# Two more pairs of k-tiles of an output projection by seven products, with three block sums made in an earlier stage

## The chip, the cores and the metric

The kernel runs on one core of a Trainium2 chip. The metric is the device time of one execution in microseconds (us). Times given for a kernel are medians of several executions; a profile shows one execution.

A core has engines that run side by side, each with its own fixed order of instructions: TensorE (PE, matmuls), VectorE (DVE), ScalarE (ACT), GpSimd (POOL) and SyncE (SP), which here issues the DMAs. An instruction waits on semaphores for what it needs, and everything behind it on its engine waits with it.

## The reference, cut to what matters

One layer of an encoder on 256 positions of width 2048, in float32. An input projection gives the inputs of a state-space mixer (SSD: a convolution over 5 positions, decays, two directions) and of a pooling mixer. Both results, 1024 wide each, go side by side through one output projection; then come a gated feed-forward stage and a gated embedding.

```python
hn = rmsnorm(h, mix_norm_pre[i])
proj = hn @ w_in[i]
z, xbc, dt_raw, u = jnp.split(proj, split_at, axis=-1)
y_ssd = ssd_mixer(z, xbc, dt_raw, ...)
y_pool = pool_mixer(u, pool_w[i], pool_scale[i])
mix = jnp.concatenate([y_ssd, y_pool], axis=-1) @ w_out[i]
h = h + rmsnorm(mix, mix_norm_post[i])
hn = rmsnorm(h, ffn_norm_pre[i])
ff = conv_glu(hn, w_ffn_up[i], ffn_conv_w[i], ffn_conv_b[i], w_ffn_down[i])
h = h + rmsnorm(ff, ffn_norm_post[i])
gate = jax.nn.sigmoid(rmsnorm(h, ple_norm_pre[i]) @ w_ple_gate[i])
h = h + rmsnorm(gate * (p[i] @ w_ple[i]), ple_norm_post[i])
```

The change concerns the product with `w_out`, which is 2048 x 2048.

## The kernel before

**Products in two parts.** Every operand of a large product is split in a rounded part and the rest (`split`, L141): ACT copies the weights to the rounded type (L152, names ending in h), DVE subtracts (L153, names ending in l). A product is then three matmuls: h by h, l by h and h by l. Weights come from DRAM into one of three buffers of 1 MB (`raw`, L156) and are split in two blocks of 1024 elements a partition. Activations are put into panels in the same two parts (`put`, L187: ACT L190, DVE L191).

**Stages.** First dt and u (dtu), then the three xbc slabs in the order 2, 0, 1 (`xbc`, L639): each multiplies 512 columns of `w_in` (`feature_major`, L323: four loads, u 0 to 3, of two blocks each), scales the result (xr, L411), does the convolution on ACT (L422) and DVE (L428, sixteen steps), and finishes with a tanh (L645) and L647. Then z, the output projection (wo), the embedding's product ple and the feed-forward stage (ug is its first weight, ga the result).

**Work laid aside.** `work` is a list of lists of small jobs; `aside` (L196) takes one list behind each load's matmuls. The lists for the slabs stand at L695 to L728: the pooling mixer (mx and mixt at L597 to L604, pw), the decays (dps and dec), the segment sums (`seg_sums`, L568: cps, seg_h L575, seg_c L576, and eight scalings seg_x and seg_w, L579 and L580), the segment matrices (`seg`, L582: two matmuls, then E by L588 on ACT, L589 on DVE, L590 on ACT), and others. The softplus of dt (sp, L530 to L541) and da come just before slab 2's lists.

**Who sets the order.** The program is written in Tile: a scheduler orders the instructions of each engine when the program is built, from the dependences, the buffers that come free and its own estimate of times; `issue_after` adds a few edges. The order in the text of the program is therefore not the order on an engine.

**Seven products.** A pair of k-tiles times a half (1024 columns) of `w_out` is a 2 x 2 product of blocks. The usual way takes eight block products, 24 matmuls of 128 x 512. `seven_products` (L239) takes seven, 21 matmuls, with sums of blocks of the weights (`add_blocks`, L232: DVE L235, L236, L237) and of the activations (`Sums`, L785, made once for each k and kept in `got`). The results gather in the usual four accumulators and four more, which `combine` (L269) adds up one pair behind the last fast one. The weights are split as a, b, c and d (L251 to L260): a and b are plain blocks, c and d hold sums. The sums are made in place in the raw buffer, or, if `block_sums` (L208) made them earlier, read back from DRAM into a page; in that case the raw buffer gets only 1536 of its 2048 columns. `block_sums` returns four lists of jobs: load, nothing, additions, store.

**The output projection.** `sublayer` (called at L852) runs two halves of 1024 columns over eight pairs, u 0 to 7, in the order k = 8, 10, 12, 14, 0, 2, 4, 6. The lower k need y, which is turned by `y_turn` (L758, four jobs set aside at L766) while the upper four pairs run. Before the change pair u 5 (k 2) of half 0 and pairs u 2 and 4 (k 12 and 0) of half 1 are fast, all three with sums in place. At the end the norm: squares on ACT (L822), products with the gain (L823), the updates of h (L830) and the new panel (wox) by PE transposes and `put`.

**Buffers.** Pages (1 MB) come from a pool of 13, raw buffers from one of 3, split parts from pools of 5.

Of the kernel before, what the change touches and what calls it, by code (L numbers as in the profile page):

```python
# [36 lines left out]
V_MIX, V_SCW, V_SCB, V_SN, V_PS, V_FN = 0, 16, 76, 88, 96, 104  # L37
# [14 lines left out]
def build(nc, a, out):  # L52
    x = a["x"][0]
    w_in, w_out, w_up = a["w_in"][0], a["w_out"][0], a["w_ffn_up"][0]
# [3 lines left out]
    with tile.TileContext(nc) as tc, \  # L58
# [12 lines left out]
        def page(name, dtype=F32):  # L71
            return gp.tile([P, 2048], dtype, tag="pg", bufs=13, name=name)
# [43 lines left out]
        def load(dst, src, ahead=False):  # L116

            with tc.issue_after(last["dma"]) if last and not ahead else nullcontext():
                return ins(nc.sync.dma_start(dst, src))
# [36 lines left out]
        def raw(name, src, a_, b_):  # L156
            r = wp.tile([P, 2048], F32, tag="raw", bufs=3, name=name)
            if src is None:
                return r
            last["dma"] = load(r[:, :a_ * b_].rearrange("p (a b) -> p a b", a=a_), src, True)  # L160
            return r
# [43 lines left out]
                yield o, c  # L205
                c += o.shape[-1]

        def block_sums(name, w, c0, k, held):  # L208


            pg = []

            def fetch():
                r = page(f"{name}b{c0}_{k}")
                pg.append(r)
                load(r.rearrange("p (k c) -> p k c", k=2),
                     w[k * P:(k + 2) * P, c0:c0 + 1024].rearrange("(k p) c -> p k c", p=P))

            def add():
                add_blocks(pg[0])  # L220
                if held:
                    sums_[name, c0, k] = pg[0], True

            def store():
                if not held:
                    t = dp.tile([P, 2048], F32, tag=f"{name}s{c0}_{k}", bufs=1, name=f"{name}s{c0}_{k}")
                    load(t, pg[0])
                    sums_[name, c0, k] = t, False

            return [fetch], [], [add], [store]  # L230

        def add_blocks(r):  # L232

            v = r.rearrange("p (b c) -> p b c", b=4)
            nc.vector.tensor_add(v[:, 0:2], v[:, 0:2], v[:, 1::2])  # L235
            nc.vector.tensor_add(v[:, 3], v[:, 3], v[:, 0])  # L236
            nc.vector.tensor_add(v[:, 2], v[:, 2], v[:, 3])  # L237
# [124 lines left out]
        def rms(name, parts, scale, n=1):  # L362

            base = EPS
            for i, q in enumerate(parts):
                m = tiny(f"{name}m{i}", n)
                nc.gpsimd.tensor_scalar(m, q, scale, base, op0=ALU.mult, op1=ALU.add)
                base = m
            r = tiny(f"{name}r", n)
            nc.gpsimd.tensor_tensor(r, m, mhalf[:, :n], op=ALU.pow)  # L370
            return r
# [71 lines left out]
        for u in range(0, NK, 2):  # L443
            r = [wp.tile([P, 2048], F32, tag="raw", bufs=3, name=f"dtur{u}") if u else r0, page(f"dtur{u + 1}")]
            for j in range(2):
                k = u + j
# [17 lines left out]
            for j in range(2):  # L464
                k = u + j
# [127 lines left out]
        cat = Panel.__new__(Panel)  # L593
# [97 lines left out]
        def job(f, *args):  # L691
            return lambda: f(*args)

        xd = {}
        work.extend([  # L695
            [],
            [job(pool_mix, 0), job(pool_mix, 1)],
            [job(pool_mix, 2), job(pool_mix, 3), job(decays), job(seg_sums)],
            [job(seg, 0), job(seg, 1)],
        ])  # L700
        bc = xbc(2)
        work.extend([
            [job(seg, 2), job(pool_map, 0), job(pool_map, 1)],
            [job(cb, bc, 0), job(cb, bc, 1), job(seg, 3)],
            [job(seg, 4), job(weigh, 0, 0), job(pool_map, 2)],
            [job(seg, 5), job(pool_map, 3)],
# [30 lines left out]
        for t in range(2):  # L737
# [13 lines left out]
            r = rms(f"yn{t}", [ss], rz[t][:, 1:2], n=2)  # L751
# [16 lines left out]
        def gload(name, src):  # L768
            g = cp.tile([P, D], F32, tag="gain", name=name)
            load(g, src.partition_broadcast(P))  # L770
            return g
# [33 lines left out]
        def sublayer(name, w, ks, get, gain, h, vnext, panel=Panel, fast=((), ()), sums=None, at=()):  # L805

            mg = [page(f"{name}m{t}") for t in range(2)]
            sq = [[], []]
            for half in range(2):

                alt = main(f"{name}s{half}") if fast[half] and half == 0 else []
                acc = [main(f"{name}a{half}{t}") for t in range(2)]
                if fast[half]:
                    alt += main(f"{name}s{half}") if half else []
                token_major(f"{name}{half}", w, half * 1024, ks, get, acc, 1, fast[half], alt, sums, at if half else ())
                for t in range(2):
                    for n in range(2):
                        q = tiny(f"{name}q{t}{half}{n}", 1)
                        junk = sp.tile([P, 512], F32, tag="junk", bufs=1, name=f"{name}j{t}{half}{n}")
                        c = slice(half * 1024 + n * 512, half * 1024 + (n + 1) * 512)  # L820
                        b = acc[t][n]
                        nc.scalar.activation(junk, b, AF.Square, accum_out=q)  # L822
                        nc.vector.tensor_mul(mg[t][:, c], b, gain[:, c])  # L823
                        sq[t].append(q)
            r = [rms(f"{name}{t}", sq[t], 1.0 / D) for t in range(2)]
            pan = panel(f"{name}x")
            for c in range(4):
                s = slice(c * 512, (c + 1) * 512)
                for t in range(2):
                    nc.vector.scalar_tensor_tensor(h[t][:, s], mg[t][:, s], r[t], h[t][:, s],  # L830
                                                   op0=ALU.mult, op1=ALU.add)
                panel_part(f"{name}x", pan, h, vnext, 4 * c, 4 * c + 4)
            return pan
# [16 lines left out]
        for t in range(2):  # L850
            load(h[t], x[t * P:(t + 1) * P, :])
        hf = sublayer("wo", w_out, list(range(8, 16)) + list(range(8)), cat, gload("gmix", a["mix_norm_post"][0]), h,  # L852
                      V_FN, Pairs, ((5,), (2, 4)), Sums("cs", cat))


        pl = [ple(0)]
# [12 lines left out]
        for i, w_ in enumerate(which[2:] + which[:2]):  # L869
            for j, jobs in enumerate(block_sums(*w_, i >= len(which) - 2)):  # L870
                work[3 * i + 2 + j].extend(jobs)
        hid = []
        for s in range(DFF // 512):
# [12 lines left out]
            for i in range(2):  # L886
                va = main(f"va{s}{i}")
                feature_pairs(f"uv{s}{i}", w_up, DFF + s * 512 + i * 256, hf, va)
                c0 = (s % 2) * 1024 + i * 512
# [188 lines left out]
```

## Time and profile before

| | |
|---|---|
| time of the kernel, median of 3 | 1123.55 us (1123.13 to 1123.63) |
| the profiled execution's own time | 1123.86 us |
| its span in the profile | 1122.1 us |
| mean granted clock of PE | 0.998 |
| DVE busy | 925.4 us |
| ACT busy | 664.3 us |
| DMA | 300.87 MB, 268 GB/s on average |

How to read the profile: a page sums up one execution. Busy times are sums over instructions. The chain that ended last is followed back from the end, at each step to what released the instruction. A row of a timeline gives the start, the length, the engine, the line of the kernel, the operation, output and inputs, and in brackets the idle time ahead of it with what ended it; equal neighbours are put in one row (x4). A matmul's length holds its latency, so the distance between starts is what one costs in a row of them. In rows of groups, "24 | 30.1, 1255 | 22.2" reads: 24 instructions, 30.1 us busy, 1255 ns each, 22.2 us of idle time ahead of them. Buffer numbers are left out of names: xb_0l is the l part of block 0 of any load of a slab.

### The profile page before, as it was taken

The page shows a single profiled execution, that of the slowest core. Times are in us where ns is not written, and L with a number is a line of the kernel's source. Part 1 is how long each engine was busy: PE and PEld are TensorE (multiplying, and loading weights), DVE is VectorE, ACT ScalarE, POOL GpSimd, SP SyncE. Part 2 cuts the span into 40 slices and gives each one's busy share as a digit, 9 for nine tenths or more (in the row PEclk, how much of TensorE's full clock was granted, in tenths as well). Part 3 has the DMA queues.
Part 4 walks back from the last instruction along what each step waited for, and adds up shares of the span by engine and source line. Part 5 has one row for each costly group of instructions (what it writes and reads, how often), then busy time and mean ns, then how long its engine had stood idle before and what let it go on. Part 6 is the DMA issues. An engine that isn't in the chain of part 4 may idle for free.

```text
span 1122.1 us, 15775 instructions
## 1 busy us (share of the span) xinstructions
PE 1109.2 (99%) x5971; PEld 957.8 (85%) x5971; DVE 925.4 (82%) x1275; ACT 664.3 (59%) x927; POOL 76.0 (7%) x86
## 2 busy tenths in 40 slices
PE   9999999999999999999999999999999999999996
PEld 8999987888888888888888888888888888888875
DVE  6478896799898877877878778878899999889795
ACT  6848663555765554454545445445577777786672
POOL 0200004200110100000000000000000000001001
PEclk9999999999999999999999999999999999999999
DMA  9853447455799989998999998987969679995673
GB/s 360 312 196 105 160 162 280 151 188 187 248 315 340 326 307 331 301 305 304 327 331 315 286 327 301 314 292 234 333 193 334 219 289 298 383 311 184 231 235 109
DMA packets 145996, 300.87 MB, mean 268 GB/s; under 512 B 5504, under 2 KB 98560, under 8 KB 137856
## 3 DMA queue, kind: packets, MB, share of 16 engines
q1 hardware_dynamic: 145360, 298.45, 78.7%
q0 software_dynamic: 272, 1.05, 0.5%
q8 instruction: 47, 0.77, 0.3%
q10 hardware_dynamic: 288, 0.36, 0.1%
q14 instruction: 29, 0.24, 0.1%
HBM read 268.38 MB, written 31.46 MB: 267 GB/s over the span
## 4 chain that ended last, share of the span: by engine, by line
PE 95%; ACT 2%; DVE 1%; issue 1%; POOL 1%; DMA 0%; POOLq 0%; DVEq 0%; ACTq 0%
PE va L87 22%; PE ga L87 21%; PE dna L87 14%; PE woa L87 7%; PE xbc L87 6%; PE gt L87 5%; PE dtu L87 4%; PE z L87 4%; PE dns L87 3%; PE dn0s L87 1%; PE dn1s L87 1%; PE ple L87 1%; PE pw L87 1%; PE yd L87 0%; PE gts L87 0%
## 5 line engine op out<-in xcount | busy, mean ns | idle before, releaser
L87 PE MATMUL ga<-wox,ug_0h 128*128 128x512 f32 x352 | 125.6, 395 | 0.0
L87 PE MATMUL ga<-wox,ug_1h 128*128 128x512 f32 x352 | 125.0, 394 | 0.0
L87 PE MATMUL va<-wox,uv_1h 128*128 128x512 f32 x352 | 124.8, 394 | 0.0
L87 PE MATMUL va<-wox,uv_0h 128*128 128x512 f32 x352 | 124.8, 394 | 0.0
L87 PE MATMUL ga<-wox,ug_1l 128*128 128x256 f32 x352 | 99.3, 282 | 0.0
L87 PE MATMUL ga<-wox,ug_0l 128*128 128x256 f32 x352 | 99.3, 282 | 0.0
L87 PE MATMUL va<-wox,uv_1l 128*128 128x256 f32 x352 | 99.3, 282 | 0.0
L87 PE MATMUL va<-wox,uv_0l 128*128 128x256 f32 x352 | 99.3, 282 | 0.0
L87 PEld LDWEIGHTS va<-wox,uv_1h 128*128 128x128 f32 x352 | 66.2, 188 | 14.8
L87 PEld LDWEIGHTS va<-wox,uv_0h 128*128 128x128 f32 x352 | 66.2, 188 | 14.8
L87 PEld LDWEIGHTS ga<-wox,ug_0h 128*128 128x128 f32 x352 | 66.2, 188 | 14.7
L87 PEld LDWEIGHTS ga<-wox,ug_1h 128*128 128x128 f32 x352 | 66.2, 188 | 14.7
L87 PEld LDWEIGHTS ga<-wox,ug_0l 128*128 128x128 f32 x352 | 66.4, 188 | 0.1
L87 PEld LDWEIGHTS ga<-wox,ug_1l 128*128 128x128 f32 x352 | 66.3, 188 | 0.0
L87 PEld LDWEIGHTS va<-wox,uv_1l 128*128 128x128 f32 x352 | 66.3, 188 | 0.0
L87 PEld LDWEIGHTS va<-wox,uv_0l 128*128 128x128 f32 x352 | 66.3, 188 | 0.0
L884 POOL TENSOR_TENSOR fc<-fc,rfb 128x1024 f32<-128x1024 f32 x11 | 28.0, 2545 | 438.6 <-ACT fc L883 438.6
L87 PE MATMUL dna<-dn_0h,hs 128*128 128x512 f32 x160 | 50.2, 394 | 0.0
L87 PE MATMUL dna<-dn_1h,hs 128*128 128x512 f32 x160 | 49.9, 393 | 0.0
L235 DVE TENSOR_TENSOR dnb<-dnb 128x1024 f32<-128x1024 f32 x24 | 30.1, 1255 | 22.2 <-DMA dnb<-w_ffn_down 22.2
L902 ACT CAST hs<-hid 128x512 fp32r<-128x512 f32 x44 | 27.1, 617 | 23.2 <-PE dna L87 16.5
L903 DVE TENSOR_TENSOR hs<-hid,hs 128x512 fp32r<-128x512 f32 x44 | 30.2, 687 | 9.8 <-ACT hs L902 9.7
(1903 smaller groups left out, 3108.2 us busy)
## 6 DMA issues: line engine op xcount, KB each, us to landing
dnb<-w_ffn_down SPq DMA_DIRECT2D x24, 1024.0 KB, 10.4
dns<-dnb SPq DMA_DIRECT2D x22, 1024.0 KB, 7.5
dn0r<-w_ffn_down SPq DMA_DIRECT2D x10, 1024.0 KB, 6.0
dn1r<-w_ffn_down SPq DMA_DIRECT2D x10, 1024.0 KB, 7.3
zr<-w_in SPq DMA_DIRECT2D x8, 1024.0 KB, 5.2
dtur<-w_in SPq DMA_DIRECT2D x14, 528.0 KB, 9.0
wo0r<-w_out SPq DMA_DIRECT2D x7, 1024.0 KB, 5.5
wo1r<-w_out SPq DMA_DIRECT2D x6, 1024.0 KB, 5.7
```

The costliest lines, as they stand in the source:

```text
L87: last["pe"] = ins(nc.tensor.matmul(o, lhsT, rhs, start=start, stop=stop, skip_group_check=True))
L235: nc.vector.tensor_add(v[:, 0:2], v[:, 0:2], v[:, 1::2])
L884: nc.gpsimd.tensor_tensor(cv.rearrange("p (f t) -> p f t", f=4), cv.rearrange("p (f t) -> p f t", f=4), rfb.unsqueeze(1).to_broadcast([P, ...
L902: nc.scalar.copy(t[:, :512], src)
L903: nc.vector.tensor_sub(t[:, 512:], src, t[:, :512].bitcast(F32))
```

## The change

`block_sums` gets a parameter for the buffer into which it loads. In the xbc slab 2, sums are made of three weight blocks of `w_out`: columns 0 with k 0 and k 2, in pages, and columns 1024 with k 0, in one of the three raw buffers. Their loads are set aside behind slab 2's first load, the additions behind the second, third and fourth, the stores to DRAM behind the third, the fourth, and slab 0's first. In the output projection pairs u 4 and 5 of half 0 and u 2, 4 and 5 of half 1 are fast. Of these five, k 0 and k 2 of half 0 and k 0 of half 1 find their sums in DRAM; k 12 and k 2 of half 1 add in place. `combine` comes behind u 6 in both halves.

```diff
-        def block_sums(name, w, c0, k, held):
+        def block_sums(name, w, c0, k, held, get=page):
...
             def fetch():
-                r = page(f"{name}b{c0}_{k}")
+                r = get(f"{name}b{c0}_{k}")
...
+        (fa, _, aa, sa), (fb, _, ab, sb), (fc_, _, ac, sc_) = (
+            block_sums("wo", w_out, c0, k, False, get) for c0, k, get in
+            ((0, 0, page), (0, 2, page), (1024, 0, lambda n: raw(n, None, 0, 0))))
         work.extend([
-            [],
-            [job(pool_mix, 0), job(pool_mix, 1)],
-            [job(pool_mix, 2), job(pool_mix, 3), job(decays), job(seg_sums)],
-            [job(seg, 0), job(seg, 1)],
+            [*fa, *fb, *fc_],
+            [job(pool_mix, 0), job(pool_mix, 1), *aa],
+            [job(pool_mix, 2), job(pool_mix, 3), job(decays), job(seg_sums), *sa, *ab],
+            [job(seg, 0), job(seg, 1), *sb, *ac],
         ])
         bc = xbc(2)
         work.extend([
-            [job(seg, 2), job(pool_map, 0), job(pool_map, 1)],
+            [job(seg, 2), job(pool_map, 0), job(pool_map, 1), *sc_],
...
         hf = sublayer("wo", w_out, list(range(8, 16)) + list(range(8)), cat, gload("gmix", a["mix_norm_post"][0]), h,
-                      V_FN, Pairs, ((5,), (2, 4)), Sums("cs", cat))
+                      V_FN, Pairs, ((4, 5), (2, 4, 5)), Sums("cs", cat))
```

Lines behind L695 of the kernel before stand four lines lower in the changed one.

## The prediction

> **What bounds the kernel now.** I read the page first (span, busy times, the chain that ended last), then the waits of TensorE (PE), then timelines of PE, VectorE (DVE) and ScalarE (ACT) around the three places that the change reaches: the first xbc slab (53 to 82 us), the output projection (205 to 288 us) and the entry of the feed-forward stage (288 to 300 us).
>
> ```profile
> span 1122.1 us, 15775 instructions
> PE 1109.2 (99%) x5971; PEld 957.8 (85%) x5971; DVE 925.4 (82%) x1275; ACT 664.3 (59%) x927; POOL 76.0 (7%) x86
> PEclk9999999999999999999999999999999999999999
> PE 95%; ACT 2%; DVE 1%; issue 1%; POOL 1%; DMA 0%; POOLq 0%; DVEq 0%; ACTq 0%
> PE dtu L108 <- POOL ident masks.py:199: 1.4, 1, 1.4
> PE seg L87 <- ACT seg_x L579: 0.7, 1, 0.7
> ```
>
> PE is busy for 1109.2 of 1122.1 us and carries 95% of the chain, so only 12.9 us of idle PE exist in all; the last two rows are from the waits of PE: its longest, at the very start, and the one wait in the xbc slabs. PEclk is the granted clock in 40 slices, full speed (9) in all. The profiled execution took 1123.86 us (the span and 1.8 us around it); the median shown is 1123.55. I sum against 1123.86 and take off the 0.31 at the end. Two consequences: a matmul that goes is worth its pitch and no more, and an instruction that PE must newly wait for costs all of that wait. No measurement of this kernel can tell less than about 0.2% (2.2 us) from no change.
>
> **What goes.** A pair of k-tiles takes 24 matmuls of 128x512 as usual and 21 by seven products. Two more pairs, 6 matmuls fewer. The rows group two matmuls each; these are the first and the last of eleven without a gap:
>
> ```profile
> 223.80 0.62 PE L87 MATMUL woa<-wo_0l,cath 128*128 128x512 f32 x2
> 228.43 0.63 PE L87 MATMUL woa<-wo_1h,catl 128*128 128x512 f32 x2
> ```
>
> 223.80 to 228.43 is ten such rows, 20 matmuls in 4.63 us, so 0.2315 each: 6 x 0.2315 = **1.39 us less**. The combination behind the fast pairs (L269) keeps its instructions. The activation sums of k 0 were needed in half 1 already and are kept, so none is new.
>
> **What is added beside it.** Three block sums: a 1 MB load, three DVE additions and a 1 MB store each, in the first slab. The kernel makes the same sums for later weights:
>
> ```profile
> L235 DVE TENSOR_TENSOR dnb<-dnb 128x1024 f32<-128x1024 f32 x24 | 30.1, 1255 | 22.2 <-DMA dnb<-w_ffn_down 22.2
> L237 DVE TENSOR_TENSOR dnb<-dnb 128x512 f32<-128x512 f32 x24 | 18.6, 774 | 0.3
> L236 DVE TENSOR_TENSOR dnb<-dnb 128x512 f32<-128x512 f32 x24 | 16.5, 686 | 0.2
> ```
>
> 1255 and twice 686 ns (L236 and L237 have one shape) are 2.6 us; consecutive DVE instructions overlap by some 0.08, so about 2.4 us a sum. The two that meet the slab in its middle are 4.7 us of DVE. The transfers, by the same kernel's sums:
>
> ```profile
> dnb<-w_ffn_down SPq DMA_DIRECT2D x24, 1024.0 KB, 10.4
> dns<-dnb SPq DMA_DIRECT2D x22, 1024.0 KB, 7.5
> ```
>
> About 10.4 us to landing and 7.5 for a store. A pre-summed pair then reads 1.75 MB where a plain pair reads 1 MB. None of that is a cost as long as nobody waits: DVE and the DMA engines have room. What decides is the order. Each engine executes one fixed order, and in the built programs that order differs far beyond the added instructions. SyncE's queue, DVE, ACT and PE are all rearranged from slab 2 to slab 0, in the output projection's first fast pair, and where the feed-forward stage begins; the z stage and the feed-forward stage behind its second slab stand as before. I price these three places by carrying the rows below through the new orders.
>
> **Place 1: slab 2 into slab 0.** DVE before:
>
> ```profile
> 67.81 0.36 DVE L548 TENSOR_SCALAR da<-da 128x128 f32<-128x128 f32 x2
> 68.09 1.22 DVE L153 TENSOR_TENSOR xb_0l<-xb0r,xb_0h 128x1024 fp32r<-128x1024 f32 x1
> 69.23 1.28 DVE L604 COPY mixt<-mx 128x512 f32<-128x512 f32 x2
> 73.61 1.23 DVE L153 TENSOR_TENSOR xb_0l<-xb0r,xb_0h 128x1024 fp32r<-128x1024 f32 x1 [1.62 <-ACT xb_0h L152]
> 78.67 0.74 DVE L576 SCALAR_TENSOR_TENSOR seg_c<-seg_h,small,cps 64x512 f32<-64x512 f32 x1 [2.64 <-ACT seg_h L575]
> 87.02 0.69 DVE L589 TENSOR_TENSOR E<-seg,E 128x512 f32<-128x512 f32 x1 [3.79 <-ACT E L588]
> 87.64 1.77 DVE L428 SCALAR_TENSOR_TENSOR cv<-xr,vt,cv 128x254 f32<-128x254 f32 x4
> 89.93 4.82 DVE L428 SCALAR_TENSOR_TENSOR cv<-xr,vt,cv 128x255 f32<-128x255 f32 x12
> ```
>
> Before, all of slab 2's weights were split ahead of the first of these rows, and xb_0l of slab 0's first two blocks at 68.09 and 73.61, far ahead of their use. In the new order the six additions stand between the steps of the softplus chain (sp, L539 to L541) and da, in place of four splits of 1.14 us pitch (68.09 to 69.23); 4.7 against 4.6 us, so da still ends at 68.1. But the first mixt copy (now ahead of a split) and the split of slab 2's block 2 come only then: mixt to 68.8, xb_0l to 70.0. SyncE also sends slab 2's last two blocks later, the third behind DVE's split of block 0 at 56, the fourth behind the store of the first sum; by the 10 us of these rows both land before DVE turns to them.
>
> ```profile
> 66.64 0.37 PE L87 MATMUL xbc<-hnh,xb_0h 128*128 128x256 f32 x1
> 82.33 0.28 PE L87 MATMUL xbc<-hnh,xb_0h 128*128 128x256 f32 x1
> 82.57 0.28 PE L87 MATMUL xbc<-hnh,xb_0l 128*128 128x256 f32 x1
> 92.08 2.00 PE L87 MATMUL pw<-mixt,poolw 128*128 128x256 f32 x8
> ```
>
> PE starts that block at 66.64, has four matmuls (0.12 each, 82.33 to 82.57 for two) and three of mx (0.3) that it can do, and stands still until 70.0: 2.6 us late. Everything that follows from slab 2 shifts: dps, cps, then on ACT
>
> ```profile
> 78.06 0.58 ACT L575 CAST seg_h<-cps 64x512 fp32r<-64x512 f32 x1 [1.24 <-PE cps L87]
> 80.50 0.72 ACT L579 ACTIVATE seg_x<-seg_c,small 32x512 fp32r<-32x512 f32 x1
> 85.65 0.72 ACT L580 ACTIVATE seg_w<-seg_c,small 32x512 fp32r<-32x512 f32 x1
> 86.40 0.59 ACT L588 COPY E<-seg 128x512 f32<-128x512 f32 x1
> ```
>
> seg_h, eight scalings of 0.73 us from 80.50 to the one that starts at 85.65, and the first E copy at 86.40. In the new order no split stands between seg_h and the eight, so they begin when DVE has made seg_c (78.67 + 0.74 + 2.6 = 82.0) and run to 87.9. E is copied at 87.9 and DVE's minimum (L589, 87.02 before) comes at 88.5. Now the new order bites: DVE has the split of slab 0's **first** block behind that minimum, a second one and 15 of slab 2's 16 convolution steps (L428). From the rows above 16 steps take 6.4 us, 0.40 each. So 88.5 + 0.7 + 0.4, the second minimum (it waits for PE and ACT) to 90.4, 14 x 0.40 = 5.6 to 96.0, and the split to **97.2**. Before, PE used xb_0l at 82.57. Between those times PE can do only what the new order puts ahead: six seg products (128x512, 0.23 each as above, 1.4 us), four matmuls instead of two (0.24), four pool products (half of the eight at 92.08, 0.8): 2.4 us. The wait of 0.7 in the first fence goes. 97.2 - 82.6 - 2.4 - 0.7 = **11.5 us lost**, the 2.6 at the block before included. Behind it DVE is about where it was before, PE 11 us later, so slabs 0 and 1 cost nothing more. The ends of this term: 2.6 if the conv steps don't delay the split, 15 if the sums land several us late.
>
> **Place 2: half 0's first fast pair.** PE, ACT and DVE:
>
> ```profile
> 223.25 0.71 PE L87 MATMUL woa<-wo_0h,cath 128*128 128x512 f32 x2
> ```
>
> ```profile
> 224.90 0.85 ACT L190 ACTIVATE cath<-yt,vt 128x256 fp32r<-128x256 f32 x2
> ```
>
> ```profile
> 225.64 0.87 DVE L191 SCALAR_TENSOR_TENSOR catl<-yt,vt,cath 128x256 fp32r<-128x256 f32 x2
> 226.43 1.22 DVE L153 TENSOR_TENSOR wo02cl<-wo02r,wo02ch 128x1024 fp32r<-128x1024 f32 x1
> ```
>
> Before, pair 0 was plain and its splits were long done. Now it is fast, and its third and fourth splits (c and d) stand behind all eight puts of the turned y (the last ones at 224.90 on ACT and 225.64 on DVE). PE starts the pair at 223.25 and has nine matmuls, to 225.3. ACT gets to c at 225.5 and ends it at 226.5, DVE at 227.6; d follows a microsecond behind each. PE waits about 1.2 for c and 0.4 for d: **1.6 us** (0 if the puts run earlier, 3 if the sum is read late, since its read stands behind two later weights in SyncE's queue). Half 1 has its splits in time; none there.
>
> **Place 3: entry of the feed-forward stage.**
>
> ```profile
> 283.49 1.22 DVE L153 TENSOR_TENSOR ug_0l<-ug00r,ug_0h 128x1024 fp32r<-128x1024 f32 x1 [1.31 <-ACT ug_0h L152]
> 290.07 0.74 DVE L830 SCALAR_TENSOR_TENSOR h<-wom,wo0r,h 128x512 f32<-128x512 f32 x1
> 292.71 0.87 DVE L191 SCALAR_TENSOR_TENSOR wox<-woxt,vt,wox 128x256 fp32r<-128x256 f32 x2
> ```
>
> ```profile
> 293.70 1.05 ACT L152 CAST ug_1h<-ug00r 128x1024 fp32r<-128x1024 f32 x1
> ```
>
> ```profile
> 293.96 0.39 PE L87 MATMUL ple<-ple_1h,ptl 128*128 128x512 f32 x1
> 294.19 0.39 PE L87 MATMUL ga<-wox,ug_0h 128*128 128x512 f32 x1
> 299.96 0.28 PE L87 MATMUL ga<-wox,ug_1l 128*128 128x256 f32 x1
> ```
>
> Before, DVE split the first up-projection block (ug_0l) at 283.49, ahead of the norm's work. In the new order that split stands behind eight h updates and six wox puts. ACT's half of the third and fourth put stands behind a split (the one at 293.70) that needs the ple accumulator, free when the last ple product (293.96) ends at 294.35: 295.4, puts to 296.2, DVE's to 296.7, two h updates (0.66 each) to 298.0, two more puts to 298.8, the split to 300.0. Before, PE had done 5.8 us of the stage by then (294.19 to 299.96 and on); now it can do two ga matmuls and eight transposes, 1.2 us. **4.6 us lost** (2.5 to 6).
>
> **Sum.** -1.39 + 11.5 + 1.6 + 4.6 = +16.3; 1123.86 + 16.3 - 0.31 = **1139.9 us**, 1.4% slower.
>
> **The rivals.** (a) Not slower: the orders differ but every late split still lands under PE. Mechanism and place: at the border the split of slab 0's first block would have to end by 85 us, when PE leaves slab 2; that needs DVE's minimum and 14 convolution steps to be over 12 us sooner than I have them. For it: PE is 99% busy, DVE 82%. Against: the steps need slab 2's own result, so they can't start before 85. Time: 1123.55 - 1.39 = 1122.2. The Trainium skill, "Perfetto Trace Analysis", Identifying Performance Opportunities, says that kernels generally gain by improving the most-contended engine; by that rule, with PE at 99% here, this is the outcome. Chance 0.08 (0.03 of it below 1121.3, should the 0.7 us wait of before go as well).
>
> (b) The border's conv steps don't hold PE, the other places do: 2.6 + 1.6 + 4.6 - 1.39 = +7.4, 1131. It needs E's first copy earlier than I think, by work that I place on ACT too late. 0.12.
>
> (c) The added transfers bind: a load of 1 MB took 10.4 us among others, and if SyncE's fourth block of slab 2, queued behind a store that waits for DVE, lands 6 to 8 us late, the whole of place 1 moves with it: 1146 to 1148. 0.12.
>
> (d) PE's clock falls in the pauses. Place 1 leaves PE mostly idle from 85 to 97. If the clock halved there, the first 24 matmuls behind it would take up to 2.8 us more: 1141 to 1142.5. The longest wait in this trace is the 1.4 us of the first fence, and the granted clock is full in every slice, so no row here shows it. The Trainium skill, "TensorE: Matmul & The Clock Gate", What's actually happening, has the clock at half after about 3.4 us of idleness and back after as much work; that would be some 1.7 us, an estimate from that page. The pauses in place 1 are broken by seg and pool products. 0.08.
>
> **How the numbers follow.** The forecast has 0.60, with 1134 to 1145 from the ends of the terms. The range 1128 to 1148 holds it and (b), (c), (d); out of it lie (a) and tails of (b) and (c), under 0.2. Faster by over 0.2%: 0.03; within: 0.05; slower: 0.92.
>
> **What would show it.** Right: PE waits of several us at xbc for the split L153 on DVE between 85 and 98; slab 0's first xb_0l near 96, behind L428; one of 2 to 3 us at 67 to 70; about 1.6 us at the first fast pair (some 11 us later than before) and 4 to 5 us of waits at ga for ug_0l; woa stage 6 matmuls shorter. Wrong: xb_0l of slab 0 before the L428 steps, PE busy 99% as now, or a wait that DMA rows end.

## The result and the profile after

The changed kernel takes 1141.14 us (median of six, 1140.34 to 1143.53) against 1123.30 us (six, 1123.13 to 1123.63) of the kernel before: 1.0158 times as long, with a 95% interval of 1.0148 to 1.0168, or 17.8 us more. The forecast was 1139.9 us, with a range of 1128 to 1148.

The page of the changed kernel (span, busy times, granted clock, the chain that ended last); the profiled execution took 1141.55 us:

```profile
span 1139.8 us, 15805 instructions
PE 1116.0 (98%) x5965; PEld 958.5 (84%) x5965; DVE 934.1 (82%) x1285; ACT 667.8 (59%) x931; POOL 76.0 (7%) x86
PEclk9998999999999999999999999999999999999999
PE 88%; DVE 4%; ACT 3%; DMA 2%; issue 1%; POOL 1%; POOLq 0%; DVEq 0%; ACTq 0%
```

PE has six matmuls less (5965 for 5971), as the change says, and yet it is busy 6.8 us longer. Most of that is the clock, visible as the 8 in the fourth slice (85 to 114 us): finer windows show PE at a granted clock of 0.50 from 86.7 to 97.0 us and from 312.0 to 315.4 us, and busy for 11.3 us of these 13.7, so some 5.6 us of its busy time are the halving. The span grew by 17.7, so PE's idle time went from 12.9 to 23.8 us, and the chain now steps over DVE, ACT and a DMA where PE carried 95% of it.

The waits of PE in the changed kernel (total, times, longest, in us):

```profile
PE ga L87 <- DVE ug_0l L153: 2.5, 1, 2.5
PE xbc L87 <- ACT xb_0h L152: 1.8, 1, 1.8
PE wos L87 <- ACT wo00ch L152: 1.5, 1, 1.5
PE seg L87 <- ACT seg_x L579: 1.4, 1, 1.4
PE dtu L108 <- POOL ident masks.py:199: 1.4, 1, 1.4
PE woxt L380 <- DVE wox L191: 1.2, 1, 1.2
```

All but the one for ident are new or longer, and they lie at the three places of the forecast: slab 2 into slab 0, the first fast pair, the entry of the feed-forward stage. To size the places I take when PE starts each stage (first matmul of that name in the timelines by tile, us):

| PE starts | before | after | shift |
|---|---|---|---|
| slab 2 | 53.39 | 53.31 | -0.1 |
| z | 143.10 | 152.67 | +9.6 |
| output projection (woa) | 199.3 | 208.9 | +9.6 |
| transposes of the new panel (woxt) | 291.0 | 302.3 | +11.3 |
| va, end of the first feed-forward block | 320.6 | 337.9 | +17.3 |
| end of the span | 1122.1 | 1139.8 | +17.7 |

So place 1 cost 9.6, the output projection 1.7 net, the entry 6.0, and everything behind it 0.4. But 16 products of ple (the embedding's product) now stand ahead of the first woxt, where before there were 14. These two, of 0.23 us each, moved 0.5 us of work from the entry into the row above it; counted where they belong, place 2 cost 1.2 net and place 3 cost 6.5.

**Place 1.** DVE's timeline of the changed kernel; the lines answer to those at 68.09 and 89.93 of before:

```profile
66.53 0.36 DVE L548 TENSOR_SCALAR da<-da 128x128 f32<-128x128 f32 x2
...
67.41 1.22 DVE L153 TENSOR_TENSOR xb_0l<-xb2r,xb_0h 128x1024 fp32r<-128x1024 f32 x1
...
88.12 5.60 DVE L428 SCALAR_TENSOR_TENSOR cv<-xr,vt,cv 128x255 f32<-128x255 f32 x14
93.64 1.22 DVE L153 TENSOR_TENSOR xb_0l<-xb0r,xb_0h 128x1024 fp32r<-128x1024 f32 x1
```

The split of slab 0's first block, at 68.09 before, now stands directly behind fourteen convolution steps and ends at 94.86. PE in the same stretch, then the windows of the granted clock (after PE's busy time and count):

```profile
84.56 0.73 PE L87 MATMUL seg<-seg_x,seg_w 128*128 128x512 f32 x2 [1.43 <-ACT seg_x L579]
...
88.26 0.79 PE L87 MATMUL seg<-seg_x,seg_w 128*128 128x512 f32 x1 [0.36 <-DVE E L589]
90.83 0.58 PE L87 MATMUL xbc<-hnh,xb_0h 128*128 128x256 f32 x1 [1.78 <-ACT xb_0h L152]
...
92.26 3.78 PE L87 MATMUL pw<-mixt,poolw 128*128 128x256 f32 x8 [0.20 <-ACT E L588]
95.48 0.78 PE L87 MATMUL xbc<-hnh,xb_0l 128*128 128x256 f32 x1
```

```profile
core 0: us, PE busy (x) PEld busy (x) DVE busy (x) ACT busy (x) POOL busy (x), PEclk, DMA share, GB/s
82.00:86.00 4.00, 1.94 (x13) 1.30 (x11) 1.48 (x3) 3.89 (x7) 0.00 (x0) 1.00 0.75 282
86.00:88.00 2.00, 1.67 (x3) 0.64 (x3) 1.50 (x3) 2.00 (x4) 0.00 (x0) 0.68 0.02 6
88.00:92.00 4.00, 1.96 (x5) 1.22 (x5) 4.00 (x11) 3.83 (x7) 0.00 (x0) 0.50 0.00 0
92.00:96.00 4.00, 3.79 (x10) 3.02 (x10) 4.00 (x8) 3.05 (x4) 0.00 (x0) 0.50 0.00 0
```

PE does seg and pool products, as foreseen, but at half the clock from 88 on: the eight pool products of 2.00 us before take 3.78, and the clock is full again only at 97.

None of PE's waits here ends on the split of slab 0's first block. From 83 to 92.3 us they come to 4.6 us; four of the six end on ACT (seg_x, E, xb_0h), two on DVE's minimum for E. The chain that ended last runs mostly over ACT up to 92.2: the scalings, the first copies of E, two of ACT's own convolution steps (L422), the casts xb_0h and xb_1h and the next copy of E, which the pool products wait for. Behind that it is PE itself. The split ends at 94.86, and PE is busy with pool products at half clock until it starts xb_0l at 95.48, 0.6 us later.

**Place 2.** PE at the first fast pair, and ACT's split ahead of it:

```profile
236.62 0.50 PE L87 MATMUL wos<-wo00ch,csp 128*128 128x512 f32 x1 [1.47 <-ACT wo00ch L152]
236.96 0.40 PE L87 MATMUL wo0s<-wo00ch,csp 128*128 128x512 f32 x1
237.57 0.50 PE L87 MATMUL woa<-wo00dh,cath 128*128 128x512 f32 x1 [0.21 <-ACT wo00dh L152]
```

```profile
235.52 1.04 ACT L152 CAST wo00ch<-wo00t 128x1024 fp32r<-128x1024 f32 x1 [0.92 <-DMA wo00t<-wos]
```

ACT was done with the puts 0.92 us earlier and waited for the sum itself: its read was issued at 225.90, behind later weights, and took 9.55 us. The first two rows show something else: the first matmul behind a gap has 0.34 us to the next, where one in a row has 0.23.

**Place 3.** PE, then DVE, at the entry:

```profile
307.54 1.06 PE L380 MATMUL woxt<-ident,h 128*128 128x128 f32 x8 [1.17 <-DVE wox L191]
311.08 0.51 PE L87 MATMUL ga<-wox,ug_0l 128*128 128x256 f32 x2 [2.48 <-DVE ug_0l L153]
```

```profile
302.81 0.75 DVE L834 SCALAR_TENSOR_TENSOR h<-wom,wo1r,h 128x512 f32<-128x512 f32 x1 [0.81 <-POOL wo1r L370]
...
309.02 0.87 DVE L191 SCALAR_TENSOR_TENSOR wox<-woxt,vt,wox 128x256 fp32r<-128x256 f32 x2
309.81 1.21 DVE L153 TENSOR_TENSOR ug_0l<-ug00r,ug_0h 128x1024 fp32r<-128x1024 f32 x1
```

The split ug_0l stands behind the h updates and six puts and ends at 311.0. That is 11.0 later than the 300.0 of the forecast, which was counted on the times of before, and the stage itself begins 11.3 later.

### The profile page after: what moved, and what is told of

The parts are those of the page before. It is cut to its first block, busy times and chain, and to the rows that moved or that the text cites. A ratio compares the mean times of both kernels' runs of the same rounds, so it can differ in the third digit from the quotient of the medians.

```text
span 1139.8 us, 15805 instructions
## 1 busy us (share of the span) xinstructions
PE 1116.0 (98%) x5965; PEld 958.5 (84%) x5965; DVE 934.1 (82%) x1285; ACT 667.8 (59%) x931; POOL 76.0 (7%) x86
## 4 chain that ended last, share of the span: by engine, by line
PE 88%; DVE 4%; ACT 3%; DMA 2%; issue 1%; POOL 1%; POOLq 0%; DVEq 0%; ACTq 0%
PE va L87 22%; PE ga L87 21%; PE dna L87 14%; PE gt L87 5%; PE xbc L87 5%; PE woa L87 4%; PE dtu L87 4%; PE z L87 4%; PE dns L87 3%; PE dn0s L87 1%; PE dn1s L87 1%; DMA wo00t<-wos 1%; PE pw L87 1%; DMA ug00r<-w_ffn_up 1%; PE ple L87 0%
```

## The experiments

The theory (A): the work and the transfers of the sums cost nothing; three changes in the order of splits on DVE and ACT do, each by itself. The rivals: the sums' own DVE time or transfers (B); a mere shortage of raw buffers, since the third sum sits in one (C); the clock (D). Each run is compared with the kernel before on the same chip (1123.38 to 1123.46 us there).

### The sums made, but not read: sums_alone

```diff
+        sums_.clear()
-                      V_FN, Pairs, ((4, 5), (2, 4, 5)), Sums("cs", cat))
+                      V_FN, Pairs, ((5,), (2, 4)), Sums("cs", cat))
```

> The three sums are made and stored as in the changed kernel, but the output projection is that of before and reads none of them. Theory A (three places, each with its own instruction order): only place 1 is left, and here the order of every engine is the changed one from slab 2 to slab 0 and the old one in the output projection and behind it. In the changed kernel the first z product starts 9.6 us later than before, so 1123.3 + 9.6 = 1133 us, with the split of slab 0's first block ending near 95 and PE's granted clock at half for some 10 us. Theory B (the 9 MB of added transfers cost, wherever they fall): here 6 of the 9 MB are left, and two thirds of the 17.8 us would be 12: 1135 us, with waits that DMA rows end. If the loss came from the output projection instead: 1123.

Measured: 1132.44 us, 1.0079 (1.0062 to 1.0095), +9.0. Slab 2's start to z takes 98.1 us (before 89.7, changed kernel 99.4), and from z on the stages last as before. Place 1 is a cost of the first stage alone, whatever the projection does with the sums.

### One more pair of half 1, sums in place: half1_pair_in_place

Against the kernel before:

```diff
-                      V_FN, Pairs, ((5,), (2, 4)), Sums("cs", cat))
+                      V_FN, Pairs, ((5,), (2, 4, 5)), Sums("cs", cat))
```

> Before, with one more fast pair (k 2) in half 1, sums in place; no early sums, nothing else. Theory A: place 1 stands as before; place 3 has the changed order (the split of the first up-projection block behind eight h updates and six puts), which in the changed kernel costs 5.8 us between the first ga and the first va product; three matmuls go (0.7). So 1123.3 + 5.8 - 0.7 = 1128.4 us. Theory B (transfers): nothing added, so 1122.6.

Measured: 1130.52 us, 1.0060 (1.0045 to 1.0075), +7.1, with no sum in the xbc slabs at all. Its waits of PE:

```profile
PE ga L87 <- DVE ug_0l L153: 2.5, 1, 2.5
PE woxt L380 <- DVE wox L191: 1.4, 1, 1.4
```

The same waits as in the changed kernel: place 3 belongs to half 1's third fast pair alone. The total is 2.1 us above the 1128.4 expected, so the 0.7 us that its three matmuls save is not to be seen; where the 2.1 are is not shown (the profiled execution, 1129.95, was the lowest of the four).

### One more pair of half 0, sums in place: half0_pair_in_place

```diff
-                      V_FN, Pairs, ((5,), (2, 4)), Sums("cs", cat))
+                      V_FN, Pairs, ((4, 5), (2, 4)), Sums("cs", cat))
```

> Before, with one more fast pair (k 0) in half 0, sums in place instead of made early. Places 1 and 3 have the order of before. Theory A: the price is that of the pair alone: -0.7 for three matmuls, and a wait at its third and fourth splits; in place DVE has 2.4 us of additions between them, so 2 to 4 us: 1124.6 to 1126.6. If sums in place were hidden: 1122.6.

Measured: 1125.37 us, 1.0016 (1.0006 to 1.0025), +1.9. The waits are for wo02ch (0.8) and wo02dh (0.7): now the second pair is late. Alone, the three parts give 9.0, 7.1 and 1.9, in sum 18.0; the change has 17.8. (In place and from DRAM are not the same form of the pair, so the agreement of the last term is partly luck.)

### The sums' jobs moved into the z stage: sums_in_z

```diff
-            [*fa, *fb, *fc_],
-            [job(pool_mix, 0), job(pool_mix, 1), *aa],
+            [],
+            [job(pool_mix, 0), job(pool_mix, 1)],
...
-            [],
+            [*fa, *fb],
...
-            [],
-            [],
-            [job(weigh, 1, 0)],
-            [job(xs_turn, xb, 1), job(weigh, 1, 1)],
+            [*aa, *fc_],
+            [*sa, *ab],
+            [job(weigh, 1, 0), *sb, *ac],
+            [job(xs_turn, xb, 1), job(weigh, 1, 1), *sc_],
```

> The changed kernel with its three sums made five lists of jobs later: loads behind the last block of slab 1, additions and stores in the first blocks of z. The orders of slab 2 and slab 0 are those of before; those of the output projection and the feed-forward entry are the changed ones. Theory A: place 1's 9.6 us go, the rest stays: 1141.1 - 9.6 = 1131.5 us. Theory B (transfers): the same 9 MB, so 1141, or more since z reads 8 MB itself.

Measured: 1139.57 us, 1.0140 (1.0125 to 1.0155): a miss. Place 1 is gone (z starts at 142.2), but z lasts 61.7 us where it lasted 53.4. PE and DVE there:

```profile
173.02 1.22 PE L87 MATMUL z<-z_0l,hnh 128*128 128x512 f32 x2 [4.67 <-DVE z_0l L153]
```

```profile
164.08 5.48 DVE L657 SCALAR_TENSOR_TENSOR w<-cbm,dt,w 128x128 f32<-128x128 f32 x8
169.49 1.21 DVE L668 TENSOR_TENSOR xd<-xs,dec 128x1024 f32<-128x1024 f32 x1
170.62 1.21 DVE L661 TENSOR_TENSOR E<-E,w 128x1024 f32<-128x1024 f32 x1
171.76 1.21 DVE L153 TENSOR_TENSOR z_0l<-zr,z_0h 128x1024 fp32r<-128x1024 f32 x1
```

The split that PE waits for (171.76) stands behind jobs that before stood behind it or between more splits. It is a late split again, at another place; 3.3 us of the lateness come from two of the eight L657, which ran beside GpSimd (last section). Behind the 4.67 us wait the clock is at 0.50 for 3.4 us more. The run also teaches that moving the jobs of a list moves the splits around them.

### Slab 0's first split ordered ahead of the convolution: split_first

```diff
...
+            if slab == 2:
+                r = raw("xb0r0", w_in[:512, DSSD:DSSD + 512].rearrange("(k p) c -> p k c", p=P), 4, 512)
+                for j in range(2):
+                    ready[f"xb00_{j}"] = split(f"xb00_{j}", r[:, j * 1024:(j + 1) * 1024], 1024)
             sc = times_rows(f"xr{slab}", acc, rxb)
-            cv = conv(f"cv{slab}", sc, 5, V_SCW + 4 * slab, 12, V_SCB + 4 * slab)
+            with tc.issue_after(last["dve"]) if slab == 2 else nullcontext():
+                cv = conv(f"cv{slab}", sc, 5, V_SCW + 4 * slab, 12, V_SCB + 4 * slab)
```

> The changed kernel, with DVE and ACT told to split slab 0's first load ahead of slab 2's convolution; sums, transfers and everything else as changed. Theory A (the convolution steps ahead of the split hold PE): the split of the first block ends near 87.5 where it ended at 94.9, and PE goes on 7 us earlier, without the pause in which its clock halves (1.4): 1141.1 - 8 = 1133 us; a little of it may come back because the convolution ends later. Theory B (the first load of slab 0, issued at 70.4 behind a store, lands late): no change, 1141.

Measured: 1137.39 us, 1.0123 (1.0108 to 1.0138), where 1133 was expected. DVE there:

```profile
86.94 1.23 DVE L153 TENSOR_TENSOR xb_0l<-xb0r,xb_0h 128x1024 fp32r<-128x1024 f32 x1 [0.38 <-ACT xb_0h L152]
...
90.03 6.39 DVE L428 SCALAR_TENSOR_TENSOR cv<-xr,vt,cv 128x254 f32<-128x254 f32 x16
```

The split ends 6.7 us earlier and slab 2's start to z takes 94.5 us, 3.6 less than in sums_alone and 4.9 less than in the changed kernel. Half of the loss goes; 1.3 of it comes back as a new wait of ple for ple_1l. Of the 4.8 that stay, 2.0 are pauses of PE that it did not have before (the two longest, 1.42 and 0.62, end on ACT's seg_x and E), and up to 1.7 are the half clock, from 87.2 to 90.6; the rest is not placed. So the place of this split is shown as the cause of half of the loss. The edit moves both halves of it, DVE's and ACT's (xb_0h, which now ends near 86.9 and not at 90.78), so it does not show on which of the two engines the order counts. That ACT's order is what remains is argued, not shown.

### PE kept busy in the pauses of place 1: kept_busy

47 matmuls of 128x256 (counted in the trace; the expectation said 65) into an accumulator that nobody reads, each tied behind the last product of PE:

```diff
...
+        def keep_warm(n):
...
+            for _ in range(n):
+                with tc.issue_after(last["pe"]):
+                    mm(idle[0][:, :L], hn(0)[0][:, :P], hn(0)[0], True, True)
...
+            if i == 0:
+                keep_warm(14)
...
+            keep_warm((5, 4, 16)[i] if i < 3 else 0)
...
+            keep_warm(8 if g == 0 else 0)
```

> The changed kernel with 65 matmuls more of 128x256 whose results nobody reads, put by hand into PE's pauses between 82 and 96 us. Clock theory: PE's granted clock stays full there; the eight pool matmuls take 1.65 us again where they took 3.8, and slab 0 goes on when its split is there: 1.4 us less, 1139.7, or up to 1 us less still since the scheduler now puts two convolution steps ahead of the E copies. If the clock had nothing to do with it: 1141, or more by what the added matmuls hold up.

Measured: 1139.71 us, 1.0145 (1.0129 to 1.0160), 1.4 less than the changed kernel. The clock stays at 1.00 in every window from 82 to 100:

```profile
91.83 1.89 PE L87 MATMUL pw<-mixt,poolw 128*128 128x256 f32 x8
...
94.18 0.39 PE L87 MATMUL xbc<-hnh,xb_0l 128*128 128x256 f32 x1
```

```profile
92.91 1.22 DVE L153 TENSOR_TENSOR xb_0l<-xb0r,xb_0h 128x1024 fp32r<-128x1024 f32 x1
```

Here PE starts xb_0l at 94.18, directly behind the end of the split at 94.13; the added matmuls fill PE almost up to there. So with the clock kept it is the late split that PE goes on from, as forecast; with the clock halved, PE comes to it later than the split ends.

Slab 2's start to z takes 98.0 us. That is 1.3 less than in the changed kernel, but no less than the 98.1 of sums_alone, whose clock fell too, and came back near 94 and not at 97 (pw there 3.24 us). So in place 1 the order costs 8.3 us and the clock between 0.1 and 1.3, by when it returns: half clock costs nothing while PE would wait for the split anyway. Two caveats: here three convolution steps stand ahead of the first minimum for E and one fewer ahead of the split, and place 2's wait was 0.4 and not 1.5, so the total alone does not show it.

### The entry's splits ordered early: entry_split_early

Against the changed kernel, the first splits of ple and ug are made ahead of half 1's products with the gain:

```diff
...
+                early_split = name == "wo" and half == 1
...
-                        nc.vector.tensor_mul(mg[t][:, c], b, gain[:, c])
+                        with tc.issue_after(last["dve"]) if early_split else nullcontext():
+                            nc.vector.tensor_mul(mg[t][:, c], b, gain[:, c])
...
+            if early_split:
+                ready["ug000_1"] = split("ug000_1", r_[:, 1024:], 1024)
```

> The changed kernel with the splits of ple's and of the feed-forward stage's first block made ahead of the gain products on DVE. Theory A: place 3's loss of 5.8 us goes, less up to 2 for the turned h, which now stands behind the ple products: 1135.4 to 1137.4 us, and no wait of PE for ug_0l. If the late landing of that weight (issued at 288.6, 295.8 on ACT) is what binds: 1141.

Measured: 1136.97 us, 1.0123 (1.0107 to 1.0138), 4.2 less than the changed kernel. No wait for ug_0l is left; from the first woxt to va are 31.5 us (before 29.6, changed kernel 35.6). Not all of these 4.2 us are gained: eight ple products more than in the changed kernel (24 for 16) now stand ahead of the first woxt, and from woa to there are 94.9 us where there were 93.4. From woa to va the gain is 2.7 us. The other 1.5 of the difference of the profiled executions lie ahead of woa, 1.0 of them in place 1, and do not belong to the edit. What stays at the entry are waits for wox of 1.1 and 0.6.

### All repaired together: all_three_repaired

sums_in_z and entry_split_early in one kernel, and in the queue of SyncE later weights behind the reads of the sums:

```diff
-            last["dma"] = load(r[:, :a_ * b_].rearrange("p (a b) -> p a b", a=a_), src, True)
+            with tc.issue_after(last["t"]) if "t" in last else nullcontext():
+                last["dma"] = load(r[:, :a_ * b_].rearrange("p (a b) -> p a b", a=a_), src, True)
...
-                    last["dma"] = load(t, sums_[stage, c0, k0][0], True)
+                    last["dma"] = last["t"] = load(t, sums_[stage, c0, k0][0], True)
```

> Five fast pairs with the sums made in z, the entry's splits early and the reads of the sums ahead of later weights in SyncE's queue. Theory A: 1123.3 - 1.4 + about 1 for the c split behind the puts + 0 to 2 at the entry: 1123 to 1125 us; better than before only if both small terms are under 0.7. Theory B: 1141.

Measured: 1137.01 us, 1.0126 (1.0109 to 1.0143): a miss of 12 us or more. The entry's 29.9 us from woxt to va look like the 29.6 of before, but ten ple products more stand ahead of woxt; from woa to va are 123.9 us, where there were 121.3 before and 129.1 in the changed kernel. No wait for ug_0l is left and c's wait falls to 0.4. But z lasts 60.6 us with 4.3 us of waits for z_0l: the part taken over from sums_in_z still costs 7 us in that stage, and a late wait of 0.7 for gt_0l is new (two_sums_half0 shows where it is from).

### The third sum in a page: three_sums_in_pages

sums_alone with one edit more:

```diff
-            ((0, 0, page), (0, 2, page), (1024, 0, lambda n: raw(n, None, 0, 0))))
+            ((0, 0, page), (0, 2, page), (1024, 0, page)))
```

> As sums_alone (nothing of the output projection changed, no sum read), but the third sum is loaded into a page too, so slab 2 keeps its three raw buffers. The six, now nine additions stand later among the softplus steps, and the split of slab 0's first block still stands behind 15 convolution steps. Theory A (that place in DVE's order is the price): about as sums_alone, 1130 to 1133 us, PE's clock halved again. Theory of the raw buffer (two instead of three starve slab 2 and cause the loss): 1123.5 to 1125.

Measured: 1132.92 us, 1.0086 (1.0072 to 1.0100). DVE's split of slab 0's first block starts at 93.19, behind fourteen convolution steps again. Theory C falls: it is not the raw buffer.

### Two sums alone: two_sums_alone

sums_alone without the third sum:

```diff
-            [*fa, *fb, *fc_],
+            [*fa, *fb],
...
-            [job(seg, 0), job(seg, 1), *sb, *ac],
+            [job(seg, 0), job(seg, 1), *sb],
...
-            [job(seg, 2), job(pool_map, 0), job(pool_map, 1), *sc_],
+            [job(seg, 2), job(pool_map, 0), job(pool_map, 1)],
```

> As sums_alone with only the two sums of half 0 (pages). In this program DVE splits slab 0's first two blocks ahead of the convolution, as before the change, though six additions and 4 MB of transfers are still there. Theory A: no long pause of PE at the border, 1123.4 to 1125 us. If the sums' own work and transfers cost in proportion: two thirds of sums_alone's 9.0, 1129.4.

Measured: 1123.62 us (ten), 0.9999 (0.9990 to 1.0008): two thirds of the work and of the transfers for nothing. DVE:

```profile
76.47 1.23 DVE L153 TENSOR_TENSOR xb_0l<-xb0r,xb_0h 128x1024 fp32r<-128x1024 f32 x1 [1.42 <-ACT xb_0h L152]
79.40 1.21 DVE L153 TENSOR_TENSOR xb_0l<-xb0r,xb_0h 128x1024 fp32r<-128x1024 f32 x1
...
87.42 1.77 DVE L428 SCALAR_TENSOR_TENSOR cv<-xr,vt,cv 128x254 f32<-128x254 f32 x4
```

Both splits stand ahead of the convolution. The cost does not grow with the number of sums (0, then 9 us for the third); theory B falls for two sums, and for the third only its own load and store of 1 MB each and its 2.4 us of DVE could be such a part.

### Two sums, read by half 0: two_sums_half0

two_sums_alone with the reads put first as in all_three_repaired, and two fast pairs in half 0:

```diff
-        sums_.clear()
-                      V_FN, Pairs, ((5,), (2, 4)), Sums("cs", cat))
+                      V_FN, Pairs, ((4, 5), (2, 4)), Sums("cs", cat))
```

> The two sums of half 0, both of its pairs k 0 and k 2 fast from them, half 1 as before, reads of the sums ahead of later weights in SyncE's queue. Orders of places 1 and 3 are those without a late split. Theory A: -0.7 for three matmuls and 0.6 to 1.5 for the c split behind the eight puts: 1123.2 to 1124.5 us.

Measured: 1125.18 us (eleven), 1.0014 (1.0005 to 1.0023), 0.7 above the range expected. Waits in place 2 are 0.4 and 0.2; from woa to ga are 95.5 us (before 94.9). The rest is at a fourth place, the norm ahead of the gate (gt). DVE before, then here:

```profile
1017.63 1.23 DVE L153 TENSOR_TENSOR gt_0l<-gt0r,gt_0h 128x1024 fp32r<-128x1024 f32 x1
```

```profile
1019.65 0.74 DVE L835 SCALAR_TENSOR_TENSOR hb<-dnm,dn0r,hb 128x512 f32<-128x512 f32 x1
...
1027.86 1.22 DVE L153 TENSOR_TENSOR gt_0l<-gt0r,gt_0h 128x1024 fp32r<-128x1024 f32 x1
```

The same exchange as at place 3: the split went from ahead of the updates of the residual to behind them, and PE waits 0.7 us for it. From the first down product (dna) to the last gt are 321.9 us where there were 320.5. All three kernels with that edge on the weights' loads have this wait and none of the others has; that the edge causes it was not tried by itself.

### The same, with y turned earlier: two_sums_early_y

```diff
-        work.extend([[], [], [job(y_turn, 0), job(y_turn, 2)], [job(y_turn, 4), job(y_turn, 6)]])
+        work.extend([[], [], [job(y_turn, 0), job(y_turn, 2), job(y_turn, 4), job(y_turn, 6)], []])
```

> As two_sums_half0, with all four turns of y set aside in one list, one pair earlier, so that the puts end about 2 us sooner ahead of the c split. Theory A: the wait at c goes: 1123.4 - 0.7 = 1122.7 us, at best level with before or 0.06% under it. If the puts bind elsewhere (PSUM's two small buffers): 1124 or more.

Measured: 1124.56 us (eleven), 1.0011 (1.0002 to 1.0019). From woa to ga are 95.0 us, so half 0's pair is down to no loss and no gain; the wait for wo00cl is 0.4, and the late stage costs its 1.6 (322.1 us from dna to the last gt). The 1122.7 hoped for was missed. No version beat the kernel before.

## Why the prediction was right

The sign, the three places and the total held: 17.7 us in the profile where the sum had 16.3. The mechanism held in the main (a few splits or casts gone late in the new orders), but not in each step, and that the total came so close is partly luck: the terms' errors cancel. Of the signs named as right, the late split at 93.64 behind L428 came; a wait of several us for it at xbc, and one of 2 to 3 us at 67 to 70, did not.

- **Six matmuls less, -1.39.** The count is right. The gain is hidden everywhere: new waits at the pairs eat it; no total of half1_pair_in_place or two_sums_early_y shows it.
- **Place 1, 11.5 forecast, 9.6 measured**, in the end by another sum. What failed is the step "4.7 against 4.6 us, so da still ends at 68.1", with its 2.6 us at the block before: da ends at 66.9, and PE waits there only 0.4 in all. I had exchanged four splits for six additions of that length and overlooked that DVE had stood idle among those splits, as this row of the kernel before shows:

```profile
63.62 1.23 DVE L153 TENSOR_TENSOR xb_0l<-xb2r,xb_0h 128x1024 fp32r<-128x1024 f32 x1 [1.36 <-ACT xb_0h L152]
```

  The additions fill that hole. So E's first copy came at 85.28 (forecast 87.9) and the split ended at 94.86 (97.2). From there on the step held: 15 of 16 convolution steps ahead of the split, 5.60 us for fourteen. Of PE's work in the gap I had counted half of the pool products; all eight stand there. That PE would stand and wait for this split is not what the profile shows: it is held by ACT up to 92.3 and by its own half clock up to 95.48, and only with the clock kept does it go on right behind the split's end (kept_busy). The order alone is worth 8.3 us there; the clock brings the profile to 9.6.
- **Place 2, 1.6 forecast, 2.6 measured** (1.2 net and the 1.39): the c and d splits are late as forecast, but what ACT waited for was not the puts. It is near the end of the term, "3 if the sum is read late": the read took 9.55 us behind two later weights. With the reads put first c's wait was 0.4. Waits are 1.5 and 0.2 of it. The slow first matmul behind each gap, 0.1 each, is a part of the rest; about 0.7 us I can't place.
- **Place 3, 4.6 forecast, 6.5 measured.** The order was right and half1_pair_in_place isolates it. The waits are 4.1 us (2.48, 1.17 and one of 0.47 for h, behind a POOL step); the clock, at 0.50 from 312.0 to 315.4, is some 1.7 us, which I had not priced there. The 0.7 left are not placed.
- **The rivals.** (a) had every late split land under PE: the waits above refute it; the busiest engine had less to do, and the kernel got slower. (b), which left only 2.6 of place 1, falls by sums_alone, where place 1 by itself costs 9.0. (c), the transfers, falls by two_sums_alone and by the fact that no long wait in place 1 ends on a DMA; in place 2 a read is late, for 0.9 us of ACT. (d), the clock, to which I gave 0.08, came true beside the forecast and not in its place. Its own time, 1141 to 1142.5, is that of the median, but by chance: without the 2.6 that failed it would lie lower. Where I argued that seg and pool products break the pauses and so keep the clock, that was wrong.

What stays open: what makes the order flip at the third sum and at the third fast pair. The runs show that it does, and what it costs, not which estimate or buffer tips it; a page instead of the raw buffer did not flip it back. In place 1 it is also open how much belongs to DVE's order and how much to ACT's. Nor was any repair of place 1 found that holds back all of its 8.3 us.

## What to carry to other kernels

Where a scheduler orders the engines, price a change first by the new orders, engine by engine, and look for a split or a cast that has gone behind a long row of work that itself waits for the stage before; six matmuls in 6000 are worth 1.4 us, one such split 5 to 8. When a row of work is exchanged for another of the same length, look for idle time between its pieces before taking the end as unchanged. And a repair that adds an order edge or moves jobs must be read as a new order too: two of mine moved a loss of this kind to another stage.

## What the runs showed of the hardware

**The clock falls without one long pause.** From 82 to 92 us of the changed kernel PE was busy 5.6 of 10 us, in pieces, with no wait over 1.8 us; the granted clock was 0.68 from 86 and 0.50 from 88 to 96, and full from 97. In sums_alone, with nearly the same pieces, it came back near 94. Finer windows give the length of the half clock: 10.2 us in the changed kernel (86.7 to 97.0), 6.8 in sums_alone (87.5 to 94.3) and in three_sums_in_pages (88.1 to 95.0), 3.4 in split_first (87.2 to 90.6) and at the entry of the changed kernel. These are three, two and one times 3.4 us. In the 3.4 us ahead of each of these falls PE was busy for 0.9 to 2.2 us, in the 3.4 us ahead of each return for 3.2 us or more. The Trainium skill, "TensorE: Matmul & The Clock Gate", What's actually happening, tells of a monitor with a free-running window of about 3.4 us: that the same order gets its clock back at different times agrees with it. Its summary, Why this matters for your kernels, warns of idle gaps over some 3 us; here pauses of 1.8 us at most, close together, did the same. One wait of 4.67 us in sums_in_z did it too.

**DVE and GpSimd in each other's way.** In sums_in_z eight instructions of L657 took 5.48 us (the row at 164.08 above) beside GpSimd operations of L672 (the first row here); in the kernel before, with GpSimd idle, they took 2.18 (the second):

```profile
159.39 8.45 POOL L672 TENSOR_TENSOR y<-xs,small 128x1024 f32<-128x1024 f32 x2 [83.00 <-ACT w L654]
```

```profile
159.55 2.18 DVE L657 SCALAR_TENSOR_TENSOR w<-cbm,dt,w 128x128 f32<-128x128 f32 x8
```

The Trainium skill, "SBUF — State Buffer", SBUF: two separate sides, says that a VectorE operation with two inputs in SBUF and a GpSimd operation that reads SBUF exclude each other for a whole instruction. The rows agree with that. The 3.3 us more are two of the eight, of 1.99 us each instead of 0.34, and each ends 0.15 us behind the end of one of GpSimd's two operations. GpSimd's first took 6.5 us and its second 1.9: during most of the first, VectorE's rows ran at their usual length. No run here takes the GpSimd operation away.
